# Two weight blocks at a time in the seven products: the order of the matmuls within a step

## The chip, the cores and the metric

The kernel runs on one core of a Trainium2 chip. The metric is the device time of one execution in microseconds (us). A core has a matrix engine (PE; its weight loads stand apart as PEld), a vector engine (DVE), a scalar engine (ACT), a general engine (POOL), and a queue engine (SP) that issues most DMAs. Each engine runs its own instructions in the order in which they stand in its program, and semaphores tie them together: an instruction that waits holds up all that stand behind it on its engine.

## The reference, cut to what matters

One layer of a decoder trunk for 1024 tokens of width 1024, in float32:

```python
def reference(x, c, positions, ...):
    mod = (silu(c) @ w_ada + b_ada)[:, None, :]
    sh1, sc1, gt1, sh2, sc2, gt2 = split(mod, 6)
    h = rmsnorm(x, g_mix) * (1 + sc1) + sh1
    proj = h @ w_in                      # 1024 x 4640: queries, keys, values, latents, gates
    ...
    merged = sigmoid(gate_a) * (attention_a @ w_up_a) + sigmoid(gate_b) * (attention_b @ w_up_b)
    x = x + gt1 * (merged @ w_o)
    h = rmsnorm(x, g_ffn) * (1 + sc2) + sh2
    x = x + gt2 * ((silu(h @ w_gate) * (h @ w_up)) @ w_down)
    return rmsnorm(x, g_final)
```

Three large products matter here: the input projection `h @ w_in`, the gate and up projections `h @ w_gate` and `h @ w_up` (1024 by 2816 each), and the down projection `... @ w_down`.

## The kernel before

Activations lie transposed: features on the 128 partitions, tokens along the free dimension, in two halves of 512 tokens. To keep the accuracy of float32 with the fast matmul format, each operand is split into a rounded part and a remainder ("hi" and "lo"), and each product of two tiles is three matmuls into one accumulator bank: hi by hi, hi by lo, lo by hi. A split is two instructions (`split`, lines 82 to 84): ACT rounds (a CAST, line 83), then DVE or POOL subtracts (line 84).

**Strassen.** The three large products run in Winograd's form: the weights of a block (256 outputs by the whole depth, four quarters) and the activations (four quarters, made once by `Rights` and shared by all blocks) give seven products in place of eight. A `Strassen` object is one weight block. Its products run in the order 0, 1, 5, 4, 6, 3, 2 (`ORDER`, line 170, also `OR`). `left(i)` forms the weight operand of product i, where needed by sums on POOL (line 189), and splits it into one of six weight tiles (`Wop`). `product` (line 211) then runs nk times three matmuls of 128 by 128 weights against a 128 by 512 right operand: nk is 4 in the input projection and in gate/up, 2 in the down projection. So a product is 12 or 6 matmuls, all into one bank.

A block uses three banks, "a", "b" and "c". Products 0, 5, 6 and 3 all accumulate in "a", product 1 goes to "b", products 4 and 2 to "c". Between two of those in "a" the sum so far is read out: after product 0 by `keep` (line 160, an ACT COPY at line 162; in the down projection line 1219), after 5 and 6 by `plus` (line 228), which is `keep` again or, where the block has a `base` sum from earlier, a DVE add (line 232). The next product into "a" can begin only when that read is done. `done` combines a finished bank with such sums, and goes on to the next stage.

**Pairs.** Blocks run in pairs: two of `In` in the input projection (line 700, nine pairs; in the first four both blocks have a `base`), gate and up of `Pair` (line 1118, eleven pairs, two blocks called g and u), two of `Down` (line 1211, ten pairs). Within a pair a step is one product of the first block, then the same product of the second.

**What sets the order.** The code is not the order of the engines: a scheduler places the instructions of each engine by priority and by its own estimate of when operands are ready. It fills in, for example, the first matmuls of the next pair's product 0 ahead of a product that it expects to wait. The reads `u2` and `u3` after products 5 and 6 are given priority (`tc.high_priority`).

The core of a step before:

```python
def product(self, i, name, start):
    w = self.left(i)
    ...
    for k in range(self.nk):
        for n, (wi, ti) in enumerate(((0, 0), (0, 1), (1, 0))):
            PE.matmul(ps, w[:, wi, k], t[k][:, ti], ...)
```

Of the kernel before, what the change touches and what calls it, by code (L numbers as in the profile page):

```python
# [44 lines left out]
def layer_kernel(ctx: ExitStack, tc: tile.TileContext, xT, c, pos, relT, wada, bada, gains, gq, gkv,  # L45
# [3 lines left out]
    ACT, DVE, PE, POOL, SP = nc.scalar, nc.vector, nc.tensor, nc.gpsimd, nc.sync  # L49
# [32 lines left out]
    def split(src, hi, lo, eng=DVE):  # L82
        ACT.copy(hi, src)  # L83
        eng.tensor_sub(lo, src, f32(hi))  # L84
# [80 lines left out]
    HP = 400  # L165

    class Strassen:
        """Winograd's form for one 256 by 1024 block of outputs."""

        ORDER = (0, 1, 5, 4, 6, 3, 2)  # L170

# [36 lines left out]
            split(src, w[:, 0], w[:, 1])  # L208
            return w.rearrange("p l (k f) -> p l k f", f=P)

        def product(self, i, name, start):
            w = self.left(i)
            if start:
                self.bk[name] = bank()
            ps = self.bk[name]
            t = self.T[i]
            for k in range(self.nk):
                for n, (wi, ti) in enumerate(((0, 0), (0, 1), (1, 0))):
                    PE.matmul(ps, w[:, wi, k], t[k][:, ti], start=start and k == 0 and n == 0,  # L219
                              stop=k == self.nk - 1 and n == 2, skip_group_check=True)  # L220

        def pre(self, copy, done):
            self.product(0, "a", True)
# [8 lines left out]
            DVE.tensor_add(t, ps, self.base)  # L232
            return t

        def step(self, i):
            if i == 0:
                self.product(0, "a", True)
                self.s1 = self.keep(self.bk["a"], (0, 0))
            elif i == 1:
                self.product(1, "b", True)  # L240
                self.done((0, 0), self.bk["b"], self.s1)
            elif i == 5:
                self.product(5, "a", self.base is not None)
                with tc.high_priority(offset=HP):
                    self.u2 = self.plus(self.bk["a"], (0, 1))
            elif i == 4:
                self.product(4, "c", True)
            elif i == 6:
                self.product(6, "a", False)
                with tc.high_priority(offset=HP):  # L250
                    self.u3 = self.plus(self.bk["a"], (1, 1))
                self.done((1, 1), self.bk["c"], self.u3)
            elif i == 3:
                self.product(3, "a", False)
                self.done((1, 0), self.bk["a"], self.base)
            else:
                self.product(2, "c", False)
                self.done((0, 1), self.bk["c"], self.u2)

    class Rights:  # L260
        """The right operands of the seven products, from tiles' halves, which they overwrite."""

        def __init__(self, tiles, nk, alloc, eng):
            self.t, self.nk, self.alloc, self.eng = tiles, nk, alloc, eng
# [133 lines left out]
    with ExitStack() as s0:  # L398
# [62 lines left out]
        for k in range(8):  # L461
            square(0, k)
            if k == 0:
                for hf in range(2):
                    ACT.activation(crow[hf], crow[hf], AF.Silu)
                    st(cnd[:, hsl[hf]], crow[hf])
                    ps = bank()
# [17 lines left out]
        for k in range(8):  # L485
# [18 lines left out]
            t = R1.ops[k // 4][k % 4]  # L504
# [6 lines left out]
            for j in range(NGP):  # L511
                s = slice(j * P, j * P + P)
                if k == 6 and j == 2:
                    gates.enter_context(tc.issue_after(rows_ins[0].ins))
                for n, (wi, ti) in enumerate(((hi, 0), (hi, 1), (lo, 0))):
                    PE.matmul(pss[j], wi[:, s], t[:, ti], start=k == 0 and n == 0, stop=k % 4 == 3 and n == 2,
                              skip_group_check=True)
            kr_mm(hi[:, NGP * P:], t, k == 0, k == 7)
            if k == 3:
                for j in range(NGP):  # L520
                    t = SG()
# [15 lines left out]
    prs = [In(j, load=False, base=sg[j]) for j in range(NGP)]  # L537
# [3 lines left out]
    t = cell(4, dt=F32)  # L541
    for j in range(2):
        prs[4 + j].out((0, 0), pss[4 + j], None, lambda: t[:, j])
    for j in range(4):
        t = cell(j)
# [33 lines left out]
    for j in range(4):  # L579
        t = cell(8 + j)  # L580
# [4 lines left out]
    for j in range(4):  # L585
        t = R1.ops[2][j]
        kr_mm(kw[:, 4 + j], t, False, j == 3)
    t, tmp = X2()
# [111 lines left out]
    for g in range(9):  # L700
        pair = [prs[p] if p < 8 else In(p) for p in (2 * g, 2 * g + 1)]
        for q in pair:
            if q.pr < 8:
                q.load()
            if q.pr == 7:
                q.base = X()
                ld(q.base, spq)
        gates.close()
        for i in OR:
            for q in pair:  # L710
                if i > 1 or q.base is None:
                    q.step(i)
            for ch in chores:
                ch.at(7 * g + OR.index(i))
    assert all(ch.n == len(ch.items) for ch in chores)
# [2 lines left out]
    with ExitStack() as s2:  # L718
# [40 lines left out]
        anchor = [None]  # L759

        class Unit:
            """Queries 256 I to 256 I + 255 of one head."""

            def __init__(self, hd, I, osum, row, idx):
                self.hd, self.I, self.osum, self.row, self.idx = hd, I, osum, row, idx
# [246 lines left out]
        for u in range(64 + DEPTH):  # L1012
# [11 lines left out]
            w = u - DEPTH  # L1024
            if sc:
                spend(units[u].scores(sc.pop(0)))
            for kp in range(w % 4 + 1) if w >= 0 else ():
# [4 lines left out]
                if len(queue) > 2:  # L1032
                    q, k = queue.pop(0)
# [16 lines left out]
    def wload3(src, n):  # L1050
        raw = WP.tile([P, 16, P], F32, name="Wraw")[:, :8]
        hi = WO.tile([P, 8, P], F32R, name="Wop")
        lo = WO.tile([P, 8, P], F32R, name="Wop")
        ld(raw[:, :n], src.rearrange("p (k f) -> p k f", f=P))
        split(raw[:, :n], hi[:, :n], lo[:, :n])
        return hi, lo
# [3 lines left out]
    for j in range(8):  # L1060
        w = wload3(wupb[j], 4)
# [56 lines left out]
    class Pair:  # L1118
# [37 lines left out]

        def steps(self, ids):
            for i in ids:
                self.g.step(i)
                self.u.step(i)  # L1160

    p0 = Pair(0)
    p0.steps(OR[:1])
# [30 lines left out]
    def load_act(f):  # L1194
        t = cell(next(rcell), dt=F32)
        t = [t[:, 0], t[:, 1]]
        ld2(t, actd[f])
        return t

    def dsplit(f0, nk):  # L1200
        R = Rights([load_act(f0 + j) for j in range(2 * nk)], nk, TT, lambda j: DVE)
        R.early()
        R.late()
        return R.ops
# [25 lines left out]
    for ci in range(NC):  # L1230
        for dd in range(2):
            prs = [Down(ci, 2 * dd + e, ops) for e in range(2)]
            if dd == 1:
                if ci < NC - 1:
                    nxt = dsplit(4 * ci + 4, 2)
                else:
                    tail = []
                    for f in (20, 21):
                        raw = load_act(f)
                        tl = [TT(), TT()]  # L1240
                        for hf in range(2):
                            split(raw[hf], tl[hf][:, 0], tl[hf][:, 1])
                        tail.append(tl)
            for i in OR:
                for q in prs:
                    q.step(i)
        ops = nxt

    raw = WP.tile([P, 16, P], F32, name="Wraw")
# [157 lines left out]
```

## Time and profile before

| | |
|---|---|
| median of 3 runs | 1727.06 us (1724.98 to 1730.79) |
| profiled execution, from its first to its last instruction | 1721.8 us |
| mean granted TensorE clock | 0.964 |
| PE busy | 92% of the span, 7306 matmuls |
| DVE, ACT, POOL busy | 71%, 50%, 42% |
| DMA | 267.88 MB, mean 156 GB/s |

The profile is one execution. In its rows PE stands for matmuls, PEld for weight loads, "L219" for line 219, and "bk<-cell,Wop" for what an instruction writes and reads: a bank from a right operand (`cell`) and a weight tile (`Wop`). Behind an arrow "<-" in a list of waits stands the engine and line that ended the wait, then the microseconds in total, how often, and the longest. In the instructions in order of time the first number is the start, the second the length (of a merged group: from the first start to the last end), and in brackets stands how long the engine had been idle and what ended that. A matmul's row is longer than the distance to the next one, since matmuls overlap in the array. Stages by time: first norms and six weight columns to 84 us, input projection to about 460, attention to about 860, output projection to 996, gate/up to 1445, down projection to 1682, and the last block and norm.

### The profile page before, as it was taken

How to read it: one execution, taken by the hardware profiler on the slowest of the kernel's cores; microseconds unless marked ns; L12 is line 12 of the kernel's file. 1: busy time of each engine (PE TensorE's matmuls, PEld its weight loads, DVE VectorE, ACT ScalarE, POOL GpSimd, SP SyncE). 2: the span in 40 equal slices, each digit the busy share in tenths (PEclk: the TensorE clock that was granted, in tenths of full speed). 3: DMA queues.
4: the chain of work that ended last, by engine and by line, in shares of the span. 5: the costliest groups of instructions: out<-in, count | busy, mean ns of one | idle time of the engine just before them, and what ended most of it. 6: DMA issues, size and time to landing. Idle time of an engine off the chain costs nothing.

```text
span 1721.8 us, 22038 instructions
## 1 busy us (share of the span) xinstructions
PE 1581.5 (92%) x7306; PEld 1279.9 (74%) x7306; DVE 1224.3 (71%) x2335; ACT 868.4 (50%) x1703; POOL 730.1 (42%) x614
## 2 busy tenths in 40 slices
PE   5779998999879989999999989999999999888896
PEld 3557786777668877999888867888888887566675
DVE  7996659567267757889865778544444448999987
ACT  5653434434366867878733454333333345555444
POOL 4573425323343546434140226322223226667683
PEclk9989999999889999999999999999999999999998
DMA  8338447467996878765294422422222237223212
GB/s 311 141 116 286 174 151 251 156 193 225 292 231 179 222 187 209 184 166 144 67 342 150 155 80 73 150 76 99 91 93 86 92 135 250 74 74 99 73 50 98
DMA packets 156066, 267.88 MB, mean 156 GB/s; under 512 B 34845, under 2 KB 70349, under 8 KB 150705
## 3 DMA queue, kind: packets, MB, share of 16 engines
q1 hardware_dynamic: 107952, 224.45, 39.0%
q0 software_dynamic: 48000, 42.04, 11.4%
q8 instruction: 57, 0.93, 0.2%
q14 instruction: 57, 0.46, 0.1%
HBM read 195.72 MB, written 75.34 MB: 157 GB/s over the span
## 4 chain that ended last, share of the span: by engine, by line
PE 42%; DVE 13%; DMA 4%; issue 3%; ACT 2%; POOL 1%; SPq 0%; DVEq 0%; ACTq 0%; POOLq 0%
PE bk L219 23%; DVE Wop L84 3%; DVE cell L84 3%; PE acc L890 3%; PE S L781 3%; PE bk L87 3%; PE bk L89 3%; PE bk L88 3%; PE pv L822 2%; PE tr L803 2%; DVE x L1225 2%; DMA vbd<-ev 2%; DVE cell L277 1%; DMA Wraw<-wdown 1%; DMA x<-x1d 1%
## 5 line engine op out<-in xcount | busy, mean ns | idle before, releaser
L219 PE MATMUL bk<-cell,Wop 128*128 128x512 f32 x4056 | 986.8, 403 | 56.8 <-DVE Wop L84 23.2
L219 PEld LDWEIGHTS bk<-cell,Wop 128*128 128x128 f32 x4056 | 772.0, 192 | 265.4 <-DVE Wop L84 37.0
L189 POOL TENSOR_TENSOR Wsum<-Wraw 128x512 f32<-128x512 f32 (+1 forms) x120 | 160.5, 1339 | 457.1 <-DVE Wop L84 278.4
L84 DVE TENSOR_TENSOR Wop<-Wsum,Wop 128x512 fp32r<-128x512 f32 (+1 forms) x241 | 185.1, 775 | 99.6 <-ACT Wop L83 99.0
L83 ACT CAST Wop<-Wsum 128x512 fp32r<-128x512 f32 (+1 forms) x241 | 131.6, 550 | 227.9 <-PE bk L219 114.3
L84 DVE TENSOR_TENSOR Wop<-Wraw,Wop 128x512 fp32r<-128x512 f32 (+2 forms) x182 | 142.8, 792 | 63.1 <-ACT Wop L83 60.3
L83 ACT CAST Wop<-Wraw 128x512 fp32r<-128x512 f32 (+2 forms) x182 | 105.2, 593 | 143.4 <-PE bk L219 62.5
L781 PE MATMUL S<-cell,cell 128*128 128x128 f32 (+8 forms) x480 | 121.2, 368 | 9.1 <-DVE mx L783 4.7
L84 DVE TENSOR_TENSOR pl<-tr,ph 128x512 fp32r<-128x512 f32 (+1 forms) x160 | 98.5, 631 | 24.8 <-ACT ph L83 23.7
L788 ACT ACTIVATE P<-P,mx 128x512 f32<-128x512 f32 (+7 forms) x128 | 99.4, 779 | 28.4 <-DVE mx L783 15.5
L890 PE MATMUL acc<-cell,w 128*128 128x512 f32 x408 | 112.8, 403 | 0.1
L1227 POOL TENSOR_TENSOR x<-x 128x512 f32<-128x512 f32 x60 | 96.2, 1610 | 37.5 <-DVE x L1225 21.7
L162 ACT COPY x<-bk 128x512 f32<-128x512 f32 x92 | 53.6, 588 | 107.1 <-PE bk L219 105.0
L803 PE MATMUL tr<-ident,P 128*128 128x128 f32 x576 | 95.6, 285 | 6.1 <-ACT P L791 5.5
L781 PEld LDWEIGHTS S<-cell,cell 96*128 96x128 f32 (+1 forms) x480 | 81.4, 198 | 18.6 <-DVE mx L783 7.8
L87 PE MATMUL bk<-cell,Wop 128*128 128x512 f32 (+1 forms) x240 | 93.4, 389 | 1.9 <-ACT Wop L83 1.9
L822 PE MATMUL pv<-ph,v 128*128 128x256 f32 (+1 forms) x320 | 89.0, 294 | 5.4 <-ACT ph L83 4.5
L83 ACT CAST ph<-tr 128x512 fp32r<-128x512 f32 (+1 forms) x160 | 83.4, 545 | 17.5 <-PE tr L803 14.2
L88 PE MATMUL bk<-cell,Wop 128*128 128x512 f32 (+1 forms) x240 | 92.2, 385 | 0.0
L89 PE MATMUL bk<-cell,Wop 128*128 128x512 f32 (+1 forms) x240 | 91.5, 384 | 0.0
L822 PE MATMUL pv<-pl,v 128*128 128x256 f32 x320 | 82.8, 293 | 4.4 <-DVE pl L84 4.0
L189 POOL TENSOR_TENSOR Wsum<-Wraw,Wsum 128x512 f32<-128x512 f32 (+1 forms) x60 | 74.5, 1243 | 27.0 <-DVE Wop L84 24.4
(264 smaller groups left out, 2410.3 us busy)
## 6 DMA issues: line engine op xcount, KB each, us to landing
Wraw<-win SPq DMA_DIRECT2D x18, 1024.0 KB, 5.9
Wraw<-wgate SPq DMA_DIRECT2D x11, 1024.0 KB
Wraw<-wup SPq DMA_DIRECT2D x11, 1024.0 KB, 6.2
actd<-x SPq DMA_DIRECT2D x44, 256.0 KB, 2.0
cell<-actd SPq DMA_DIRECT2D x44, 256.0 KB, 3.5
Wraw<-wdown SPq DMA_DIRECT2D x20, 512.0 KB, 3.6
ada<-wada SPq DMA_DIRECT2D x16, 512.0 KB, 6.1
cell<-ksd POOLq DMA_DIRECT2D x16, 512.0 KB, 21.9
```

The costliest lines, as they stand in the source:

```text
L83: ACT.copy(hi, src)
L84: eng.tensor_sub(lo, src, f32(hi))
L87: PE.matmul(ps, w[0], a[0], start=first, stop=False)
L88: PE.matmul(ps, w[0], a[1], start=False, stop=False)
L89: PE.matmul(ps, w[1], a[0], start=False, stop=last)
L189: POOL.tensor_tensor(t, a, b, op=op)
L219: PE.matmul(ps, w[:, wi, k], t[k][:, ti], start=start and k == 0 and n == 0, stop=k == self.nk - 1 and n == 2, skip_group_check=True)
L781: anchor[0] = PE.matmul(s, q[:, i * P:i * P + P], k[:, c * wd:c * wd + wd], start=pi == 0, stop=pi == len(passes) - 1)
L788: ACT.activation(t[:, :n], t[:, :n], AF.Exp, bias=mx[:, 0:1], scale=-1.0, accum_out=mx[:, 1:2])
L803: anchor[0] = PE.transpose(tr[:, co:co + P], self.p[a][:, kb * P:kb * P + P], ident)
L822: anchor[0] = PE.matmul(pv[:, o if l else 0:], v[:, kk], p[:, l:r], start=kk == 0 and n == 0, stop=last and l > 0 and n == 1, skip_group_c ...
L890: PE.matmul(ps, w[wi][:, k0 + k], act(k, ai, hf), start=k == 0 and n == 0, stop=k == nk - 1 and n == 2)
```

## The change

A step takes both blocks of a pair at once. `left` runs for both blocks first, then one loop over k runs the matmuls of both; the two reads or `done` calls follow, first block first. With e0 and e1 for the blocks, the six matmuls for one k are: e0 hi, e0 lo, e1 hi, e1 lo, each against the right operand's hi half, then e1 hi and e0 hi against its lo half. Before, they were e0 hi by hi, hi by lo, lo by hi over all k, and after these the same of e1. Nothing else is computed and nothing is left out.

```diff
+        BANK = {0: "a", 1: "b", 5: "a", 4: "c", 6: "a", 3: "a", 2: "c"}
+
+        def open(self, i, name=None, start=None):
             w = self.left(i)
+            name = name or self.BANK[i]
+            if start is None:
+                start = i in (0, 1, 4) or (i == 5 and self.base is not None)
             if start:
                 self.bk[name] = bank()
-            ps = self.bk[name]
-            t = self.T[i]
-            for k in range(self.nk):
-                for n, (wi, ti) in enumerate(((0, 0), (0, 1), (1, 0))):
-                    PE.matmul(ps, w[:, wi, k], t[k][:, ti], start=start and k == 0 and n == 0,
-                              stop=k == self.nk - 1 and n == 2, skip_group_check=True)
+            return w, self.bk[name], start
+
+        @staticmethod
+        def products(i, qs, opened):
+
+            t = qs[0].T[i]
+            nk = qs[0].nk
+            fwd = range(len(qs))
+            turns = [(e, wi, 0) for e in fwd for wi in (0, 1)] + [(e, 0, 1) for e in reversed(fwd)]
+            for k in range(nk):
+                for e, wi, ti in turns:
+                    w, ps, start = opened[e]
+                    PE.matmul(ps, w[:, wi, k], t[k][:, ti], start=start and k == 0 and (wi, ti) == (0, 0),
+                              stop=k == nk - 1 and ti == 1, skip_group_check=True)
...
-        def step(self, i):
+        def after(self, i):
             if i == 0:
-                self.product(0, "a", True)
                 self.s1 = self.keep(self.bk["a"], (0, 0))
...
             elif i == 6:
-                self.product(6, "a", False)
                 with tc.high_priority(offset=HP):
                     self.u3 = self.plus(self.bk["a"], (1, 1))
                 self.done((1, 1), self.bk["c"], self.u3)
             elif i == 3:
-                self.product(3, "a", False)
                 self.done((1, 0), self.bk["a"], self.base)
...
+        @staticmethod
+        def steps(i, qs):
+            if not qs:
+                return
+            Strassen.products(i, qs, [q.open(i) for q in qs])
+            for q in qs:
+                q.after(i)
...
         for i in OR:
-            for q in pair:
-                if i > 1 or q.base is None:
-                    q.step(i)
+            Strassen.steps(i, [q for q in pair if i > 1 or q.base is None])
...
             for i in ids:
-                self.g.step(i)
-                self.u.step(i)
+                Strassen.steps(i, [self.g, self.u])
...
             for i in OR:
-                for q in prs:
-                    q.step(i)
+                Strassen.steps(i, prs)
```

How this moves instructions is seen best where product 6 of a pair ends and product 3 follows in the same bank. PE's program before, in the middle of gate/up (a pair whose first block has bank 11569 as "a" and whose second has 11587; the right operand of product 6 is in cells 16 to 19, that of product 3 in cells 20 to 23):

```order
L219 MATMUL bk_11569<-cell18_10384,Wop_11716 128x512 x3
L219 MATMUL bk_11569<-cell19_10385,Wop_11716 128x512 x3
L219 MATMUL bk_11587<-cell16_10382,Wop_11738 128x512 [waits Activation_49]
L219 MATMUL bk_11587<-cell16_10382,Wop_11738 128x512
L219 MATMUL bk_11587<-cell16_10382,Wop_11738 128x512 [waits DVE_49]
L219 MATMUL bk_11587<-cell17_10383,Wop_11738 128x512 x3
L219 MATMUL bk_11587<-cell18_10384,Wop_11738 128x512 x3
L219 MATMUL bk_11587<-cell19_10385,Wop_11738 128x512 x3
L219 MATMUL bk_11569<-cell20_10398,Wop_11758 128x512 [waits Activation_49]
```

And of the change, the same pair (the second block's "a" is bank 11573 now; 11847 is the next pair's first bank):

```order
L232 MATMUL bk_11573<-cell18_10384,Wop_11721 128x512 x3
L232 MATMUL bk_11569<-cell18_10384,Wop_11716 128x512
L232 MATMUL bk_11569<-cell19_10385,Wop_11716 128x512 x2
L232 MATMUL bk_11573<-cell19_10385,Wop_11721 128x512 x3
L232 MATMUL bk_11569<-cell19_10385,Wop_11716 128x512
L232 MATMUL bk_11847<-cell0_9859,Wop_11844 128x512 [waits Activation_49]
L232 MATMUL bk_11569<-cell20_10398,Wop_11758 128x512 [waits Activation_49]
```

Before, the second block's twelve matmuls stand between the first block's last matmul of product 6 and its first of product 3. Now one matmul does, which is the next pair's.

ACT's program at the same place before (the copies at line 162 read the banks after product 6, the casts at line 83 round weights):

```order
L83 CAST Wop_11814<-Wsum_11812 128x512 [waits PE_49,Activation_49,Pool_49]
L162 COPY x_11731<-bk_11569 128x512 [waits PE_49]
L83 CAST Wop_11844<-Wraw_11840 128x512 [waits DMAHW4_49,DVE_49]
L1130 ACTIVATE x_11733<-x_11733 128x512 [waits DVE_49]
L162 COPY x_11753<-bk_11587 128x512 [waits DMAHW2_49,PE_49]
```

And of the change:

```order
L83 CAST Wop_11799<-Wsum_11797 128x512 [waits PE_49,Pool_49]
L83 CAST Wop_11844<-Wraw_11840 128x512 [waits DMAHW4_49,DVE_49,PE_49]
L162 COPY x_11748<-bk_11569 128x512 [waits PE_49]
L83 CAST Wop_11848<-Wraw_11842 128x512 [waits DMAHW5_49]
L162 COPY x_11753<-bk_11573 128x512 [waits DMAHW2_49]
```

The cast of the next pair's first weights has moved ahead of the first block's copy, and it waits for PE (for the second block's last matmul of product 6, whose weight tile it takes over).

In the input projection, PE's program before at the end of product 6 of a pair with a `base` (bank 1186 is the first block's "a", 1208 the second's; product 3 reads cells 8 to 11):

```order
L219 MATMUL bk_1186<-cell7_912,Wop_1265 128x512 x3
L219 MATMUL bk_1208<-cell4_909,Wop_1291 128x512 [waits DVE_49,Activation_49]
L219 MATMUL bk_1208<-cell4_909,Wop_1291 128x512 x2
L219 MATMUL bk_1208<-cell5_910,Wop_1291 128x512 x3
L219 MATMUL bk_1208<-cell6_911,Wop_1291 128x512 x3
L219 MATMUL bk_1208<-cell7_912,Wop_1291 128x512 x3
L219 MATMUL bk_1186<-cell8_925,Wop_1315 128x512 [waits DVE_49,Activation_49]
```

And of the change (the second block's bank is 1194 now):

```order
L232 MATMUL bk_1194<-cell6_911,Wop_1270 128x512 x3
L232 MATMUL bk_1186<-cell6_911,Wop_1265 128x512
L232 MATMUL bk_1186<-cell7_912,Wop_1265 128x512 x2
L232 MATMUL bk_1194<-cell7_912,Wop_1270 128x512 x3
L232 MATMUL bk_1186<-cell7_912,Wop_1265 128x512
L232 MATMUL bk_1186<-cell8_925,Wop_1315 128x512 [waits DVE_49,Activation_49]
```

Here nothing stands between the two products of the first block any more. In the down projection the program of the change keeps six matmuls or more between them, and mostly runs the matmuls of one block together, as before.

More of the change, by code (lines that the diff above doesn't have):

```diff
@@ L209, in left, with product @@
             return w.rearrange("p l (k f) -> p l k f", f=P)
-        def product(self, i, name, start):
+        BANK = {0: "a", 1: "b", 5: "a", 4: "c", 6: "a", 3: "a", 2: "c"}
+        def open(self, i, name=None, start=None):
             w = self.left(i)
+            name = name or self.BANK[i]
+            if start is None:
+                start = i in (0, 1, 4) or (i == 5 and self.base is not None)
             if start:
                 self.bk[name] = bank()
-            ps = self.bk[name]
-            t = self.T[i]
-            for k in range(self.nk):
-                for n, (wi, ti) in enumerate(((0, 0), (0, 1), (1, 0))):
-                    PE.matmul(ps, w[:, wi, k], t[k][:, ti], start=start and k == 0 and n == 0,
-                              stop=k == self.nk - 1 and n == 2, skip_group_check=True)
+            return w, self.bk[name], start
[10 more added lines that the diff above has]
+                              stop=k == nk - 1 and ti == 1, skip_group_check=True)
+        def product(self, i, name, start):
+            Strassen.products(i, [self], [self.open(i, name, start)])
         def pre(self, copy, done):
@@ L233, in plus @@
             return t
-        def step(self, i):
+        def after(self, i):
             if i == 0:
-                self.product(0, "a", True)
                 self.s1 = self.keep(self.bk["a"], (0, 0))
             elif i == 1:
-                self.product(1, "b", True)
                 self.done((0, 0), self.bk["b"], self.s1)
             elif i == 5:
-                self.product(5, "a", self.base is not None)
                 with tc.high_priority(offset=HP):
                     self.u2 = self.plus(self.bk["a"], (0, 1))
-            elif i == 4:
-                self.product(4, "c", True)
             elif i == 6:
-                self.product(6, "a", False)
                 with tc.high_priority(offset=HP):
@@ L253, in step @@
             elif i == 3:
-                self.product(3, "a", False)
                 self.done((1, 0), self.bk["a"], self.base)
-            else:
-                self.product(2, "c", False)
+            elif i == 2:
                 self.done((0, 1), self.bk["c"], self.u2)
+        @staticmethod
[5 more added lines that the diff above has]
+                q.after(i)
     class Rights:
```

## The prediction

> **What bounds the kernel now.** I read the page first, then busy time by stage, then PE's list of waits by stage, and last single instructions where the change puts a new wait.
>
> ```profile
> span 1721.8 us, 22038 instructions
> PE 1581.5 (92%) x7306; PEld 1279.9 (74%) x7306; DVE 1224.3 (71%) x2335; ACT 868.4 (50%) x1703; POOL 730.1 (42%) x614
> ...
> L219 PE MATMUL bk<-cell,Wop 128*128 128x512 f32 x4056 | 986.8, 403 | 56.8 <-DVE Wop L84 23.2
> ```
>
> The products that the change reorders are line 219: 4056 of 7306 matmuls, 986.8 of PE's 1581.5 us. PE idles 56.8 us ahead of them. The 92% is an average, so the stages have to be told apart:
>
> ```profile
> 84.00:480.00 396.00, 362.30 (x1519) 285.30 (x1519) 269.67 (x509) 164.39 (x311) 158.91 (x121) 0.94 0.65 205
> 996.00:1046.00 50.00, 43.12 (x176) 33.15 (x175) 41.80 (x56) 30.25 (x53) 22.19 (x10) 0.93 0.20 69
> 1046.00:1427.00 381.00, 381.00 (x1634) 306.50 (x1635) 194.68 (x295) 141.55 (x243) 116.45 (x84) 1.00 0.30 103
> 1427.00:1445.00 18.00, 18.00 (x79) 14.48 (x78) 15.42 (x32) 8.48 (x18) 12.08 (x5) 1.00 0.76 248
> 1445.00:1682.00 237.00, 210.10 (x834) 158.03 (x833) 220.27 (x306) 117.15 (x252) 165.42 (x136) 0.96 0.26 90
> ```
>
> Columns: length, then PE, PEld, DVE, ACT, POOL busy (with instructions), granted clock, DMA share, GB/s. Input projection (84 to 480) and gate/up (996 to 1445) are PE's; the down projection (1445 to 1682) is DVE's, 220.3 of 237 us. In gate/up PE is busy all 381 us at clock 1.00: 381 us / 1634 = 233 ns for each matmul. The lists of waits agree, for 1046 to 1440 and then for the input projection (84 to 450, the five largest of line 219):
>
> ```profile
> PE bk L219 <- DVE cell L84: 0.8, 1, 0.8
> ```
>
> ```profile
> PE bk L219 <- ACT cell L395: 4.4, 1, 4.4
> PE bk L219 <- DVE x L383: 4.2, 3, 3.1
> PE bk L219 <- DVE cell L84: 4.1, 2, 3.0
> PE bk L219 <- ACT x L162: 3.9, 3, 2.2
> PE bk L219 <- DVE x L232: 2.4, 1, 2.4
> ```
>
> So in gate/up there is no wait to win, 0.8 us in all; only a shorter spacing than 233 ns could gain there, and every new wait of PE is paid in full.
>
> **Part 1, the same half streamed again: cost 0.** Instruction counts stay: each matmul still has its own weight load, and only the order changes. Before, no two neighbours of line 219 within a product share the moving half. After, 4 of 6 matmuls stream the half that the one ahead of them streamed. The first stage of before has such neighbours: at line 516 six matmuls stream one half past six weights, and twelve then alternate the halves.
>
> ```profile
> 40.44 1.53 PE L516 MATMUL bk<-cell,gwh 128*128 128x512 f32 x6
> 41.81 0.40 PE L474 MATMUL tr<-cell,gwh 128*64 128x512 f32 x1
> 42.05 0.39 PE L516 MATMUL bk<-cell,gwh 128*128 128x512 f32 x1
> ...
> 44.33 0.39 PE L516 MATMUL bk<-cell,gwh 128*128 128x512 f32 x1
> ```
>
> One half for all: 41.81 - 40.44 = 1.37 us for 6, 228 ns each. Alternating: 44.33 - 42.05 = 2.28 us for 10, 228 ns each. Sharing the moving half shows nothing. A gain per matmul is bounded by 0 from this pair of rows and, far away, by 233 - 188 = 45 ns, since a weight load lasts 188 ns (row below) and stays; I take 0, the nearest row. I exclude no loss, but the new mixes of bank and weight stand in those twelve matmuls too, at 228 ns, so I price it at 0.
>
> The Trainium skill, "TensorE: Matmul & The Clock Gate", section "Back-to-back issue gap", gives an isolated warm spacing of N/2.4 + 2.5 ns, 216 ns for 512 columns. By it 1634 matmuls would take an estimated 353 us where this trace has 381; page and row differ, and the row decides. The section names no saving for a half that is streamed twice, which goes against this change.
>
> **Part 2, a new wait between products 6 and 3.** Both write bank "a", and between them the bank must be read: keep (line 162, ACT COPY) or plus (line 232, DVE). Before, the other block's product 6, 12 matmuls or 2.8 us, stood between. After, both blocks' product 6 end together, and product 3 of the first block is due after one other matmul (gate/up, order above), or at once. The durations:
>
> ```profile
> L219 PEld LDWEIGHTS bk<-cell,Wop x4056: 186/188/338, 84.7 to 1678.1; 128*128 128x128 f32 x194
> L219 PE MATMUL bk<-cell,Wop x4056: 387/394/796, 84.7 to 1678.3; 128*128 128x512 f32 x194
> ...
> L162 ACT COPY x<-bk x92: 562/589/611, 238.6 to 1429.7; 128x512 f32<-128x512 f32 x92
> ...
> L232 DVE TENSOR_TENSOR x<-bk,sg x14: 669/680/692, 127.3 to 221.8; 128x512 f32<-128x512 f32 x14
> ```
>
> ```profile
> 127.28 1.27 DVE L232 TENSOR_TENSOR x<-bk,sg 128x512 f32<-128x512 f32 x2
> ...
> 128.09 8.17 PE L219 MATMUL bk<-cell,Wop 128*128 128x512 f32 x24 [2.38 <-DVE x L232]
> ...
> 134.96 0.62 ACT L83 CAST x<-x 128x512 fp32r<-128x512 f32 x1 [8.10 <-DVE x L383]
> 135.48 0.62 ACT L83 CAST Wop<-Wsum 128x512 fp32r<-128x512 f32 x1
> ```
>
> ```profile
> 1201.58 0.62 ACT L83 CAST Wop<-Wraw 128x512 fp32r<-128x512 f32 x1 [4.08 <-PE bk L219]
> ...
> 1202.24 0.69 DVE L84 TENSOR_TENSOR Wop<-Wraw,Wop 128x512 fp32r<-128x512 f32 x1
> ```
>
> The second fence is this wait in the trace of before: at 127.28 the adds that free bank "a" begin, the first ends 0.68 later at 127.96, and PE restarts at 128.09: 0.13 us hand-over to PE. Between ACT and DVE it is 1202.24 - 1202.20 = 0.04. Two casts that follow each other on ACT start 0.52 apart.
>
> Gate/up, with T the start of product 6's last matmul. ACT's next instruction is not the copy but the cast of the next pair's weights; its buffer comes free with the second block's last matmul, at T - 0.23. Cast: T - 0.23 + 0.39 + 0.04 = T + 0.20. Copy, 0.52 later: T + 0.72 to T + 1.31. PE gets product 3 at T + 1.44. Undisturbed it would have come after two spacings, at T + 0.47. **Stall 0.97 us.** Behind the waiting matmul stands all of PE, in order. Nothing else is made late: the second block's product 3 stands over twenty matmuls later, its copy ends 1 us after the first. The order has this wait in ten of eleven gate/up pairs: **+9.7 us**. Bounds for one: 0.64 if the copy went ahead of the cast, 2.38 as in the row at 128.09, where the add was queued behind other DVE work.
>
> Input projection, counted in the order: a pair with product 3 at once after product 6 and a DVE add: 0.39 + 0.04 + 0.68 + 0.13 - 0.23 = 1.01. One at once with a copy: 0.92. One with one matmul and the cast: 0.97. One with one matmul and an add: 0.77. One more has PE waiting there already for weights: 0. The other four keep six or more matmuls between: 0. **+3.7 us**. Bounds: 0 if the 19 us of waits above take it up, 5 x 2.38 = 12 if adds queue.
>
> **Part 3, weights needed earlier.** The second block's halves are due at the third and fourth matmul instead of the 13th and 15th. Six weight tiles still hold three steps, and 24 matmuls (5.6 us) cover two casts (0.62) and two splits (0.69) per step: 0 where PE is full. In the down projection and at 996 to 1046, where operands come late, the new order mostly keeps one block's matmuls together, and DVE sets the time. Its instructions stay, so 0. PE's longest wait from 1445 to 1682, and DVE's:
>
> ```profile
> PE bk L219 <- DVE Wop L84: 19.6, 20, 2.8
> ```
>
> ```profile
> DVE Wop L84 <- ACT Wop L83: 8.7, 9, 2.6
> DVE x L1225 <- PE bk L219: 4.7, 5, 2.2
> ```
>
> Bounds there: DVE idles 237 - 220.3 = 17 us, a gain of 17 at most; a loss is priced in the second rival. Attention keeps its order.
>
> **Sum:** 9.7 + 3.7 = 13.4 us on the span of 1721.8, so 1735.2. The median of the runs, 1727.06, is 5.3 above that span; with the same 5.3 it is 1740.5, say **1740**.
>
> **Rivals.**
> - *It doesn't do what it says / faster.* A half streamed again could be cheaper after all. It pays for the stalls from 13.4 us / (2/3 x 3153 matmuls of both PE stages) = 6.4 ns a matmul. Halfway to the bound, 23 ns: 48 us less, 1692. For: 233 ns is well above a weight load's 188. Against: the two 228s. 0.06.
> - *Down projection later, slower still.* PE waits there for late splits. If each of twenty waits grew by one split (0.69), DVE would wait in turn for products: 14 us more, 1754. It decides as soon as PE's delay reaches line 1225, where DVE already waits 4.7 us. Against: the order there is mostly unpaired. 0.13.
> - *Given back.* The reordered down projection closes half of DVE's 17 idle us, or the input projection takes up its stalls: 13.4 - 8.5 = +5, 1732 or less, down to 1722. 0.19.
> - *Given back and more:* the full 17 us less, 1724 to 1719. For it: any new order of a stage that waits this much can go either way. 0.07.
>
> **How the numbers follow.** Forecast (1733 to 1748) 0.55. About 0.3%, 5.2 us, is what a measurement here can tell from no change: 1721.9 to 1732.2. Slower: 0.55 + 0.13 = 0.68. Same: 0.19. Faster: 0.06 + 0.07 = 0.13. The range of 8 in 10 reaches from the deep end of "given back" to near the down rival's 1754: 1724 to 1752, leaving out some 0.1 below and 0.06 above.
>
> **What would show it.** Right: from 1046 to 1427 PE waits for line 162's copy about ten times, 9 to 10 us in all, each ahead of a product 3; matmuls with no wait between still 233 ns apart; down projection as long as before within 5 us. Wrong: a spacing under 230 ns in gate/up (part 1 falls); waits of 0.3 us or 2 us there (part 2's size); or a down projection off by 10 us (part 3).

## The result, and the profile after

The changed kernel takes 1751.8 us (median of four runs, 1748.2 to 1769.1); the kernel before, run beside it, 1728.9. The ratio is 1.0164, 95% interval 1.013 to 1.0197: slower by 1.6%, some 23 us. Forecast were 1740, and slower, with 1752 as the upper end: the sign was right and the size half of what was measured.

The page of the changed kernel, span and PE. Line 219 of before is line 232 now, and its idle time (the number behind the second bar) was 56.8 us:

```profile
span 1746.4 us, 21988 instructions
...
PE 1588.0 (91%) x7306; PEld 1281.0 (73%) x7306; DVE 1245.9 (71%) x2335; ACT 857.8 (49%) x1703; POOL 739.3 (42%) x614
...
L232 PE MATMUL bk<-cell,Wop 128*128 128x512 f32 x4056 | 996.7, 406 | 74.5 <-DVE Wop L84 25.1
```

The span grew by 24.6 us. Idle time grew by 17.7, and the busy time of the same 4056 matmuls by 9.9. Both are costs, as is shown below. Busy time by stage, with each stage moved by what had been lost ahead of it (columns as in the prediction):

```profile
84.00:490.00 406.00, 365.78 (x1519) 285.79 (x1519) 272.67 (x513) 163.49 (x315) 160.04 (x122) 0.94 0.63 202
1006.00:1056.00 50.00, 42.43 (x178) 33.38 (x177) 40.96 (x58) 29.33 (x52) 22.73 (x10) 0.93 0.21 69
1056.00:1446.00 390.00, 385.70 (x1635) 306.00 (x1634) 211.39 (x293) 135.61 (x242) 123.37 (x84) 1.00 0.28 100
1446.00:1464.00 18.00, 15.67 (x61) 12.04 (x60) 12.62 (x23) 7.19 (x15) 8.95 (x4) 0.91 0.50 166
1464.00:1706.00 242.00, 214.66 (x851) 165.41 (x850) 226.95 (x316) 118.59 (x257) 169.08 (x136) 0.94 0.28 95
```

The same 1519 matmuls of the input projection take 406 us instead of 396, gate/up 390 instead of 381, and the last two rows, the end of gate/up and the down projection, together 260 instead of 255 (912 and 913 matmuls).

**Gate/up.** PE's timeline there (start, length, number of matmuls, and in brackets the idle time ahead and what ended it). Before, it was one run without a pause (the view ends at 1240):

```profile
1049.66 190.56 PE L219 MATMUL bk<-cell,Wop 128*128 128x512 f32 x816
```

After, it breaks once in each pair of blocks:

```profile
1126.28 39.54 PE L232 MATMUL bk<-cell,Wop 128*128 128x512 f32 x168 [0.48 <-ACT Wop L83]
1166.29 39.72 PE L232 MATMUL bk<-cell,Wop 128*128 128x512 f32 x168 [0.47 <-ACT Wop L83]
1206.48 39.72 PE L232 MATMUL bk<-cell,Wop 128*128 128x512 f32 x168 [0.47 <-ACT Wop L83]
```

From 1166.29 to 1206.48 are 40.19 us for 168 matmuls; 168 x 233.3 ns would be 39.19. So a pair loses 1.0 us, where 0.97 was forecast. The bracket names only the first of two waits that stand side by side. One such place in full:

```profile
1095.66 1.10 PE L232 MATMUL bk<-cell,Wop 128*128 128x512 f32 x4
...
1096.60 0.62 ACT L83 CAST Wop<-Wsum 128x512 fp32r<-128x512 f32 x1 [4.45 <-POOL Wsum L189]
1097.13 0.58 ACT L162 COPY x<-bk 128x512 f32<-128x512 f32 x1
...
1097.28 3.09 PE L232 MATMUL bk<-cell,Wop 128*128 128x512 f32 x11 [0.52 <-ACT Wop L83]
1097.76 2.40 PEld L232 LDWEIGHTS bk<-cell,Wop 128*128 128x128 f32 x11 [0.30 <-ACT x L162]
```

ACT's cast for the next pair goes first, the copy of bank "a" follows 0.53 later and ends at 1097.71; PE's single matmul of the next pair starts at 1097.28, and product 3 at 1097.76, 0.05 after the copy. The list of waits puts all of it down to the cast:

```profile
PE bk L232 <- ACT Wop L83: 4.3, 9, 0.5
```

Nine waits of 0.5 us are half of what is lost; the other half stands behind the next instruction, and is seen in the distance from break to break alone.

**Input and down projection.** PE's largest waits in the input projection (84 to 462), then from 1440 to 1706, and DVE's from 1462 to 1706:

```profile
PE bk L232 <- DVE Wop L84: 8.5, 4, 3.4
PE bk L232 <- ACT x L162: 7.6, 3, 5.5
PE bk L232 <- ACT Wop L83: 7.3, 4, 3.7
```

```profile
PE bk L232 <- DVE Wop L84: 13.6, 9, 2.9
PE bk L232 <- ACT x L1232: 11.6, 4, 4.0
```

```profile
DVE x L1238 <- PE bk L232: 8.3, 6, 2.8
...
DVE x L1152 <- PE bk L232: 4.1, 1, 4.1
```

In the input projection, waits for weights (Wop of lines 83 and 84) grew from 3.9 us to 15.8; before they were

```profile
PE bk L219 <- ACT Wop L83: 2.0, 1, 2.0
...
PE bk L219 <- DVE Wop L84: 1.9, 1, 1.9
```

In the down projection PE waits less often for DVE's splits, but now for the copy of line 1232 (line 1219 before, 0.5 us), and DVE, which sets the time there, waits 8.3 us for PE's products where it waited 4.7, and 4.1 for a product of gate/up (line 1152). All of DVE's idle time in that stage hardly grew, as is shown with the experiments.

### The profile page after: what moved, and what is told of

The parts are those of the page before. It is cut to its first block, busy times and chain, and to the rows that moved or that the text cites. A ratio compares the mean times of both kernels' runs of the same rounds, so it can differ in the third digit from the quotient of the medians.

```text
span 1746.4 us, 21988 instructions
## 1 busy us (share of the span) xinstructions
PE 1588.0 (91%) x7306; PEld 1281.0 (73%) x7306; DVE 1245.9 (71%) x2335; ACT 857.8 (49%) x1703; POOL 739.3 (42%) x614
## 4 chain that ended last, share of the span: by engine, by line
PE 43%; DVE 11%; DMA 4%; issue 3%; ACT 3%; POOL 2%; SPq 0%; DVEq 0%; ACTq 0%; POOLq 0%
PE bk L232 25%; DVE Wop L84 3%; PE acc L904 3%; PE S L795 3%; PE bk L87 3%; PE bk L88 3%; PE bk L89 3%; DVE cell L84 2%; PE pv L836 2%; PE tr L817 2%; DMA vbd<-ev 2%; DVE x L1238 2%; DVE cell L293 1%; POOL Wsum L189 1%; DMA Wraw<-wdown 1%
## 5 line engine op out<-in xcount | busy, mean ns | idle before, releaser
L83 ACT CAST Wop<-Wsum 128x512 fp32r<-128x512 f32 (+1 forms) x241 | 127.0, 547 | 283.3 <-PE bk L232 189.4
L84 DVE TENSOR_TENSOR Wop<-Wsum,Wop 128x512 fp32r<-128x512 f32 (+1 forms) x241 | 193.2, 823 | 68.7 <-ACT Wop L83 68.4
L84 DVE TENSOR_TENSOR Wop<-Wraw,Wop 128x512 fp32r<-128x512 f32 (+2 forms) x182 | 154.0, 855 | 87.1 <-ACT Wop L83 83.7
L802 ACT ACTIVATE P<-P,mx 128x512 f32<-128x512 f32 (+7 forms) x128 | 99.3, 778 | 24.6 <-DVE mx L801 14.0
L189 POOL TENSOR_TENSOR Wsum<-Wraw,Wsum 128x512 f32<-128x512 f32 (+1 forms) x60 | 83.2, 1395 | 51.8 <-DVE Wop L84 51.3
L904 PEld LDWEIGHTS acc<-cell,w 128*128 128x128 f32 x408 | 75.8, 192 | 13.8 <-DVE ev L935 0.3
```

Source lines behind the costliest of these rows:

```text
L189: POOL.tensor_tensor(t, a, b, op=op)
L802: ACT.activation(t[:, :n], t[:, :n], AF.Exp, bias=mx[:, 0:1], scale=-1.0, accum_out=mx[:, 1:2])
L904: PE.matmul(ps, w[wi][:, k0 + k], act(k, ai, hf), start=k == 0 and n == 0, stop=k == nk - 1 and n == 2)
```

## The experiments

All kernels below keep the new order inside a product, hi x hi, lo x hi, hi x lo, unless the text says otherwise. Times are medians; a ratio is to the kernel before on the same chip, with its 95% interval. Beside the times stands a count along PE's order: the 7261 matmuls of its program are numbered from 0, and the count is how much later than before the matmul of the same number starts in the profile. By stages (number 178 is the first of the input projection at 84.7 us; 1620 stands at 460.4, 4605 at 1053.4, 6214 at 1428.8 and 7260 at 1714.6):

| kernel | input projection, 178 to 1620 | gate/up, 4605 to 6214 | down projection, 6214 to 7260 | ratio |
|---|---|---|---|---|
| changed kernel | +8.6 | +11.6 | +3.4 | 1.0164 |
| e1 input alone | +6.4 | 0.0 | -3.2 | 1.0019 |
| e2 gate/up alone | -5.6 | +10.9 | +0.9 | 1.0053 |
| e3 down alone | -4.0 | 0.0 | +1.6 | 0.9968 |
| e4 none | -1.9 | 0.0 | -3.3 | 0.9942 |
| e5 all but 6 and 3 | +0.8 | 0.0 | +6.1 | 1.0021 |
| e6 only 6 and 3 | +1.2 | +10.4 | -3.4 | 1.0025 |
| e7 none, new inner order in input | +1.6 | 0.0 | -1.2 | 0.9987 |
| e8 none, new inner order in down | -4.5 | 0.0 | -4.3 | 0.9970 |
| e9 both opened, not alternating | -7.5 | 0.0 | +0.9 | 0.9937 |
| e11 none, eight weight tiles | -4.8 | +1.6 | +4.1 | 1.0014 |
| e10 as changed, eight weight tiles | +6.0 | +2.7 | +10.4 | 1.0119 |

Gate/up repeats to 0.1 us where nothing is paired and the tiles are as before. The input projection does not: seven unpaired profiles (before, e2, e3, e4, e7, e8, e11) lie between -5.6 and +1.6, with a mean of -2.7. So one profile settles nothing there that is smaller than 4 us, and the ratios have to be read with it. The down projection is little better: e4 and e9 have the same order of instructions there on every engine and lie 4.2 us apart, and the five kernels with the new inner order and nothing taken together there (e1, e2, e4, e8, e9) lie between -4.3 and +0.9.

**One stage alone, and none.** The call got a switch, set by stage:

```diff
-        def steps(i, qs):
+        def steps(i, qs, together):
...
+            if together:
                 Strassen.products(i, qs, [q.open(i) for q in qs])
                 for q in qs:
                     q.after(i)
+            else:
+                for q in qs:
+                    Strassen.products(i, [q], [q.open(i)])
+                    q.after(i)
```

> Only the input projection takes the two blocks together; gate/up and the down projection run one block after the other. Theory A (each stage's loss is its own, and the loss of the input projection is two to three times the 3.7 us forecast): 1737 to 1739, that is +8 to +10 on the kernel before, which stood at 1729. Rival B (the forecast's 3.7 us was right for this stage, and the rest of the difference seen there lies between executions: the two profiles were 1.5 us apart ahead of any changed instruction): 1732 to 1734.

> Only gate/up takes the two blocks together. Theory A (ten waits of about 1 us between product 6 and product 3, one per pair, and the last pair's of 2.7): +10 to +12 on the kernel before, 1739 to 1741. Rival B (the waits only bring forward time that the down projection would have waited anyway, since DVE bounds it): +2 to +5.

> Only the down projection takes the two blocks together. Theory A (the new order of its weights and products costs there by itself, as the traces' difference from its first to its last matmul says): +3 to +6 on the kernel before, 1732 to 1735. Rival B (that difference is carried in from the last gate/up pair, and the stage itself is as long as before, as forecast): 0, 1727 to 1731.

> No stage takes two blocks together; what stays of the change is the order inside a product, hi x hi, lo x hi, hi x lo, so that the second of three matmuls streams the half of the first again. Theory A (a half that is streamed again costs and saves nothing): within 3 us of the kernel before, 1726 to 1732, and 233 ns a matmul in gate/up. Rival B (the new inner order itself costs, whatever the pairing): more than 1737. Rival C (a repeated half saves 10 ns): a third of 4056 matmuls, 13 us less, 1716.

Measured: e1 1729.4 (1.0019, 0.9993 to 1.0044), e2 1737.6 (1.0053, 1.0034 to 1.0072), e3 1723.6 (0.9968, 0.9949 to 0.9987), e4 1721.3 (0.9942, 0.992 to 0.9965). None of the expectations for e1, e3 and e4 held as written (e2 came out 1.4 us under its theory A), for one reason: with nothing paired the new inner order alone is 0.6% **faster**. That was no theory of mine at this size, and it hid part of the change's price. Against e4 the three stages cost 0.77% (13 us), 1.11% (19 us) and 0.26% (5 us); their sum, 37 us, agrees with the whole, 1.0164 - 0.9942 = 2.2% or 38 us, within these intervals of some 4 us for each ratio. Not all of e2's 19 us are found: its profile, of the fastest of ten runs, is 11.3 us longer than e4's, with 10.9 in gate/up.

It isn't a saving per matmul: in e4 a matmul that streams the half of the one ahead into the same bank follows it after 234.8 ns (1201 such pairs), one that streams the other half of the same cell after 232.2 (1276), and in the changed kernel all kinds of neighbours, with a repeated half and with another, follow after 232 to 234.

**Is it the wait between 6 and 3?** The switch now asks for the product:

```diff
-            Strassen.steps(i, prs)
+            Strassen.steps(i, prs, i not in (6, 3))
```

and the same in the other two stages; e6 has `i in (6, 3)`.

> Five of the seven products take the two blocks together in all stages; products 6 and 3 run one block after the other, so that a block's bank is read while the other block's product stands on TensorE. Theory A (the loss is the wait between product 6 and product 3, with the half clock that follows it where it is long): the waits of gate/up are gone, most of the input projection's too, and the time comes down from 1752 to 1726 to 1733, a few us above the 1721 of the kernel that takes nothing together. Rival B (the loss is that the second block's weights are needed earlier in every product): five sevenths of the 30 us between 1721 and 1752 stay, 1740 to 1746.

> The mirror image: only products 6 and 3 take the two blocks together, the other five run one block after the other. Theory A (the wait between 6 and 3): nearly the whole loss, 1742 to 1750, with ten waits of about 1 us on the copy of line 162 in gate/up. Rival B (weights needed earlier): two sevenths of it, 1727 to 1732.

Measured: e5 1731.8 (1.0021, 1.0004 to 1.0039), e6 1732.6 (1.0025, 1.0006 to 1.0045). e5 lies in theory A's range, but e6 9 us under it and close to B's, so neither theory holds for both: each half of the change costs about as much as the other, 0.79% and 0.83% over e4. In gate/up the stages tell them apart: e5 loses 0.0 and e6 loses 10.4, so there it is the wait between 6 and 3, all of it. In the down projection it is the reverse, +6.1 and -3.4. In the input projection both lose 3 to 4 us against the mean of the unpaired profiles, which is within their spread, and all seven products together (changed kernel, e1, e10: mean +7.0) 9.7, which is outside it. PE's waits for weights there (84 to 462) are 6.2 us in e4, 6.2 in e5, 11.0 in e6 and 15.8 in the changed kernel and in e1: they grow where products 6 and 3 are among those taken together, and not with the other five alone.

**Which part of taking together?** In e9 both blocks' weights are made first and both results are read last, but the matmuls do not alternate:

```diff
-                Strassen.products(i, qs, [q.open(i) for q in qs])
+                opened = [q.open(i) for q in qs]
+                for q, o in zip(qs, opened):
+                    Strassen.products(i, [q], [o])
                 for q in qs:
                     q.after(i)
```

> In every step both blocks' weights are made first and both results are read last, as in the changed kernel, but the matmuls of the first block all stand ahead of those of the second. Its two results are asked for together, but no product alternates between the blocks. Theory E (what is left of the loss beside the wait between 6 and 3 is the alternation: PE needs the second block's weights two matmuls behind the first block's, and one late split stops both): 1721 to 1726, as the kernel that takes nothing together. Rival F (it is that the results are read later and the weights are asked for in another order): 1730 to 1740. Gate/up has no wait of 1 us per pair under either, since 12 matmuls stand between a block's product 6 and its product 3.

Measured: 1716.7 (0.9937, 0.9914 to 0.996; the profile is of the longest of its five runs). By the ratio nothing of the loss is left, and the time is even 4 us under theory E's range. But the run tells less than it was meant to: in the built kernel the scheduler put the instructions back. In the traces of e9 and e4 the operations and their operands, by name, stand in the same order on every engine, except on PE, ACT and DVE between 361 and 417 us, in the input projection. Behind that e9 is e4 run again, so F was hardly put to the test, and it stays open. PE's timeline has gate/up in one piece, as without the change:

```profile
1049.73 390.54 PE L232 MATMUL bk<-cell,Wop 128*128 128x512 f32 x1673
```

and in the down projection (1445 to 1712) DVE waits for PE's products 3.6 us (line 1245 is line 1238 of the changed kernel):

```profile
DVE x L1245 <- PE bk L232: 3.6, 5, 1.4
```

where the changed kernel had 8.3, e4 2.7 and e5 7.1. These waits are at most a part of what makes the down projection longer. Alternation can hardly be the rest, since the built order of the changed kernel has hardly any there: 6 of 143 products are broken up more than once by matmuls of another one, against 108 of 134 in gate/up and 64 of 114 in the input projection. The stage from number 6214 to the last matmul, in e4, e9, e5 and the changed kernel (columns as in the prediction; DVE's busy time stands ahead of the third bracket):

```profile
1430.00:1712.00 282.00, 247.58 (x1054) 195.21 (x1052) 259.18 (x395) 143.63 (x311) 192.24 (x152) 0.96 0.30 102
1426.00:1712.00 286.00, 250.53 (x1054) 194.24 (x1052) 261.92 (x396) 144.15 (x311) 187.02 (x152) 0.96 0.30 101
1435.00:1727.00 292.00, 251.34 (x1055) 191.29 (x1053) 268.37 (x397) 143.67 (x311) 187.97 (x152) 0.97 0.29 99
1450.00:1739.00 289.00, 252.56 (x1055) 198.69 (x1055) 263.01 (x393) 143.80 (x310) 186.81 (x152) 0.93 0.29 97
```

DVE is idle for 22.8, 24.1, 23.6 and 26.0 us of these, nearly the same. What grows from e4 to e5 is its busy time, by 9.2 of 10 us, with the same work: its 140 splits of weights take 106.4 us there, not 97.5 (98.6 in e9, 101.9 in the changed kernel). In all four kernels a split that meets no instruction of POOL takes 0.41 us, at most 0.43, and one that does 0.82 to 0.96 on average, up to 1.57. So the longer time goes with splits on DVE that run beside POOL's instructions; no run separates the two, and why the change makes it worse stays open.

**Another order in gate/up.** Eight weight tiles instead of six in gate/up and the down projection, paired (e10) and not (e11, its control):

```diff
-    WO = pool(ctx, "WO", 6)
+    WO = pool(ctx, "WO", 8)
...
-    xp = pool(ctx, "xp", 22)
+    xp = pool(ctx, "xp", 19)
```

> The changed kernel with eight weight tiles instead of six in gate/up and the down projection (and 19 instead of 22 tiles named x, to make room). In the order the next pair's product 0 then stands whole, 24 matmuls, between products 6 and 3 of a gate/up pair. Theory A (gate/up loses by the hand-over of the bank alone): the ten waits on the copy of line 162 go from about 1 us to under 0.2, 9 to 11 us; and if the six tiles were also what made the down projection later, another 4 to 8: 1733 to 1742. Rival G (the stalls of gate/up are waits on weights, which two more tiles do not make earlier): above 1746.

> The control for the one with eight weight tiles: the same tiles, nothing taken together, the new order inside a product. If the tiles alone change nothing where nothing is taken together: 1718 to 1725, as with six tiles (1721). If eight tiles help or 19 tiles named x hurt by themselves, the difference from 1721 says by how much.

Measured: e10 1751.0 (1.0119, 1.0086 to 1.0152), e11 1729.1 (1.0014, 0.9992 to 1.0036). e10's time lies in rival G's range and e11's 4 us above its own, but in gate/up the mechanism was the one of theory A. With two more tiles the next pair's product 0 stands whole between products 6 and 3, and after a few pauses in the first pairs PE runs through:

```profile
1139.32 320.92 PE L232 MATMUL bk<-cell,Wop 128*128 128x512 f32 x1373 [0.52 <-ACT Wop L83]
```

320.92 us / 1373 = 233.7 ns, no pause per pair: all seven products alternate here, and the wait is gone because something else stands in its place. G is out. What the tiles gave there they took elsewhere: the control is 0.7% slower than e4, and e10's profiled execution, the longest of its four, lost 19.5 us between numbers 1620 and 4605, in attention and the output projection, where the control lost 8.5. Why another division of the memory makes attention longer wasn't tried.

**Where the inner order gains.** As e4, but with the old inner order (hi x hi, hi x lo, lo x hi) in two of three stages:

```diff
+            if not half:
+                turns = [(e, wi, ti) for e in fwd for wi, ti in ((0, 0), (0, 1), (1, 0))]
```

> Nothing taken together; the order inside a product is hi x hi, lo x hi, hi x lo in the input projection alone, and as in the kernel before elsewhere. Theory C (the 7 us that the new inner order gave come from both the input projection, about 3, and the down projection, about 5, as the two profiles have it): 1724 to 1727, with the kernel before at 1728. Rival D (the part in the input projection was the spread between executions): 1727 to 1730. The spacing in gate/up stays at 233 ns under both.

> The same with the new inner order in the down projection alone. Theory C: 1722 to 1725, 4 to 6 us under the kernel before, won between the first and the last matmul of the down projection. Rival D (the gain needs the new order of the input projection): 1727 to 1730.

Measured: e7 1725.7 (0.9987, 0.9965 to 1.0008), e8 1723.2 (0.997, 0.9956 to 0.9984). The down projection's part is shown by the ratio, 0.30% or 5 us, and its profile has it there (-4.3, about as much as two profiles of one order differ). The input projection's part is not told from zero: both readings of e7 stay open, and its profile is even 1.6 later. Why the down projection gains was not settled: the built order of PE keeps its sequence of products, while ACT, DVE and POOL have some of their splits and sums in another order.

## Why the prediction was right in its sign and wrong in its size

**Part 1 (a half streamed again: 0): right for what it named.** The spacing is 232 to 235 ns with a repeated half and without. But the change also moved lo x hi ahead of hi x lo inside each product, and I counted that as "only the order changes". It was worth -0.6% (e4), about -10 us by the ratio, of which some 5 in the down projection: a term with the wrong size, 0.

**Part 2, gate/up (+9.7): right.** Nine pairs lost 8.7 us (numbers 4605 to 6046), 0.97 each as forecast, by the instructions forecast: the cast, the copy behind it, product 3. e5 and e10 take the wait away in two ways, and the loss goes each time (e9 does too, but its order there is that of e4). What was missing is the last pair: there the next weights are the down projection's, they come late, and PE stands 2.3 us:

```profile
1449.50 21.57 PE L232 MATMUL bk<-cell,Wop 128*128 128x512 f32 x84 [2.33 <-ACT Wop L83]
```

**Part 2, input projection (+3.7): not contradicted.** e6, with products 6 and 3 alone taken together, is 3.9 us above the mean of the unpaired profiles, though these lie 7 us apart. As a whole e6 costs 0.83% or 14 us over e4, where the two sums of part 2 make 13.4.

**Part 3 (weights needed earlier: 0): this is the step that failed.** With it, all that taking two blocks together does beside the wait between 6 and 3 was put at nothing. e5, which leaves that wait out, costs 0.79% or 14 us over e4, and by the ratios the two together cost more than their sum. Where PE is full the step was right: e5 loses nothing in gate/up. The input projection was counted as PE's, but PE was busy for only 362.3 of 396 us there before, and in the changed kernel its waits for weights are 15.8 us, against 6.2 in e4. For the down projection the step said that "the new order mostly keeps one block's matmuls together, and DVE sets the time", which is so, and then "Its instructions stay, so 0". There it failed: DVE's instructions stayed, but their time did not, 268.4 us in e5 and 263.0 in the changed kernel, against 259.2 in e4. What joins that to the change is not shown, and e5's profile (+6.1 against -3.3 in the down projection) is a single one.

The second rival had this stage later, by another way: late splits hold up PE, and DVE then waits for products at line 1225. Those waits did become 8.3 us from 4.7, but DVE's idle time as a whole is only 3.2 us above e4's in the changed kernel and 0.8 above it in e5, so that the rival's mechanism is at best a part, and its price of 14 us for the stage was too high.

So by the ratios, against the kernel before: -10 us by the inner order (0.58%), then about +14 by the wait between 6 and 3 (0.83%) and +14 by the other five products (0.79%), +18 together. The whole ratio says +28 (the medians +23). The rest, some 10 us, would be what the two losses are larger together than alone. The profiles point to the input projection (9.7 against 3.5 and 3.9); how much of it is spread between executions stays open. So the forecast of 1740 came as near as it did because two errors of opposite sign, the gain of the inner order and the cost of part 3, both put at 0, partly cancel.

**What I did not price at all is the clock.** After several of the longer pauses PE restarts at half clock. Two such stretches of the changed kernel, and what follows each (the clock is the third number from the end):

```profile
1449.80:1453.20 3.40, 3.40 (x9) 2.55 (x9) 3.40 (x7) 1.55 (x4) 3.32 (x2) 0.50 0.69 207
1453.20:1472.00 18.80, 17.86 (x77) 14.05 (x75) 13.17 (x25) 8.80 (x20) 4.07 (x6) 1.00 0.61 196
1505.60:1511.00 5.40, 5.40 (x13) 4.24 (x14) 5.40 (x9) 3.63 (x8) 2.70 (x3) 0.50 0.68 245
1511.00:1517.00 6.00, 5.10 (x22) 3.77 (x20) 6.00 (x7) 2.96 (x7) 4.11 (x4) 0.98 0.00 0
```

In them matmuls follow each other after 427 ns, not 233, which is 0.19 us lost on each. From the input projection on, the kernel before has 130 such matmuls of 512 columns (a recorded duration above 600 ns), the changed one 162, and 24 of the 32 more are in the down projection: 32 x 0.19 = 6 us. That is most of the growth of PE's busy time, which was 9.9 us, and it comes on top of the pauses themselves. It does not follow the change alone, though: in the down projection the changed kernel has 57 of them, e2, where nothing is taken together in that stage, 60, and e5, the longest of the three there, 20. The pauses of gate/up, under 1 us and 40 us apart, start no such stretch; there the clock stays at 1.00.

The Trainium skill, "TensorE: Matmul & The Clock Gate", section "What's actually happening", has the array at half clock after about 3.4 us without work and at full clock again after about 3.4 us of work, by a window that runs freely. The way back agrees with the traces (mostly 6 to 13 matmuls, 2.6 to 5.5 us), and so does the 426.7 ns a matmul of 512 columns while the array is cold, which the same page's section "Wait — 56ns, not 53.3ns?" gives. The way down doesn't need 3.4 us in one piece here: at 1505.59 the pause was 1.06 us, 2.7 us behind one of 1.96.

```profile
1502.86 1.68 PE L232 MATMUL bk<-cell,Wop 128*128 128x512 f32 x6 [1.96 <-DVE Wop L84]
1505.59 10.51 PE L232 MATMUL bk<-cell,Wop 128*128 128x512 f32 x33 [1.06 <-DVE Wop L84]
```

## What to carry to other kernels

Before two chains of work are interleaved on an in-order engine, count for each result how much other work stands between its last write and the next use of its buffer: on a full engine, as in gate/up here, the time by which that work is shorter than copy plus queue was paid in full, once per pair, and more work put between removed it. Where an engine already waits for operands, don't put a new order at nothing: everything beside that hand-over cost about as much again here. Look for the cost in busy time as well as in waits, since in the down projection the same instructions of DVE took longer while its idle time hardly changed. Read the built order and not the source: the scheduler turned the source of e9 back into nearly e4, and left the down projection of the changed kernel almost without alternation. And take a change apart before pricing it: here a reordering inside the product, not the one in the title, was worth 0.6% by itself, and the kernels that keep it and drop the alternation (e4 at 0.9942, e9 at 0.9937) beat both kernels of this case.

## What was not expected of the hardware

A pause of TensorE can cost up to twice: once as idle time, and again as half clock afterwards, 6 to 13 matmuls at 427 instead of 233 ns, 1.2 to 2.5 us. A moving half that is streamed twice in a row gave nothing: 232 to 235 ns a matmul in every mix of bank, weight and half. The same split on DVE (128 x 256) takes 0.41 us, or up to 1.57 where it meets an instruction of POOL. And where nothing is taken together in it, the input projection varies by some 7 us across these kernels, and the down projection by 4.2 between two kernels with one order there, while gate/up, where PE never waits, repeats to 0.1 (tiles as before).
